# Turning the merged branches of three column groups on VectorE and through DRAM instead of on TensorE

## The chip, the cores and the metric

One NeuronCore of a Trainium2 chip runs the whole program. The metric is the time of one execution in microseconds; the kernel before has a median of 1301.43 us over three runs (1301.05 to 1301.47). Engines are named as in the profile: PE is TensorE, ACT is ScalarE, DVE is VectorE, POOL is GpSimd, SP is SyncE (here it only issues DMAs). The program holds one list of instructions for each engine, and the listings and timelines below follow these lists.

## The reference, cut to what matters

One layer of a hybrid streaming encoder over 512 positions (S) and 2048 channels (D). Three attention branches give ys, one gating path gives gates, and the layer ends with

```python
up = jnp.einsum('bsnw,nwd->bsnd', ys, w_up)       # 3 branches, 512 -> 2048 columns each
merged = jnp.sum(gates * up, axis=2)              # (1, 512, 2048)
return x + jnp.einsum('bsd,de->bse', merged, w_out)
```

The change touches only the step between the last two lines: `merged` is produced with positions on the partitions, and the product with w_out contracts over its columns, so it must be turned (transposed) before TensorE can use it.

## The kernel before, in words

**Products.** All large products are made in float32 from pairs of rounded parts: an operand is split into a high part (ACT copies it to fp32r, lines 247 and 376) and a low part (DVE subtracts the high part, lines 251 and 386), and three products high-high, low-high and high-low are added in PSUM. All of them are issued in line 266. A *unit* is the work on one loaded piece of weights, 512 KB (`raw`, loaded on SP in line 278): ACT makes `wh`, DVE makes `wl`, PE multiplies. There are three buffers for `wh` and two for `wl`, so DVE can make the `wl` of a unit only when the unit two before it is finished.

**The stage around the change.** `up_units` (line 1312) makes the up-projection by column groups g of 512 columns, in the order 0, 2, 1, 3. In each group the branches C, B, A come one after the other, two units each, so six units to a group. A unit does its work by blocks of 128 positions (tb = 0 to 3): four products with `wh`, two with `wl`. After the second unit of a branch has finished a block, `taken` (lines 1319 to 1333) lets DVE multiply the block's PSUM bank by the gate (L1323, `sg<-acc,sg`), which also frees that bank, and, for branches B and A, add it to `merged` (L1330). There are four such banks (`acc`), one for each tb, so the first unit of the next branch can start its block tb only when L1323 of the same tb has read the bank.

**Turning.** When the four blocks of a group are merged, `turned_m` (line 1350) turns 128 columns at a time: four PE transposes into one PSUM bank (L1357), an ACT copy to SBUF (L1364, `m<-att`). Sixteen transposes and four copies to a group. The copy `m` goes to `merged_a` for groups 0 and 1 (DVE subtracts halves in L1378, then the split of lines 247 and 251) or to `merged_b` for groups 2 and 3 (DVE L257 several times, then splits). After the four groups, `out_task` makes the product with w_out in a Strassen form, whose operands are these splits.

**What sets the order.** The order on PE, ACT and DVE is fixed while the program is built, by a planner (`Flow`, line 65). Every piece of work is a generator that yields what it waits for and what it costs on which engine; the planner keeps a clock for each engine, takes the piece that could start first, and the instructions are recorded in that order (`manual_schedule`). SP's and POOL's DMAs are recorded when the planner passes them. Three rules of it matter here. A generator that yields an `Event` whose time is already known runs on at once, with its own `ready` set to that time. `spawn(gen, slack, ready)` starts a new generator with the `ready` that it is given. `flow.fin` is the end of the piece of work that was planned last. At run time nothing of the planner is left but the order; each instruction waits on semaphores for what it really needs.

**DMA semaphores.** DMAs on SP use eight semaphores in turn (DMAHW0 to DMAHW7 in the listings), and a DMA waits for the one before it on its semaphore.

**A round trip that the kernel has already.** `gate` (line 913) turns the 128x512 gate tile of a head with four DVE transposes of 128x128 (L920, each in blocks of 32x32), one store to DRAM (L923, `gd<-gt`) and four loads issued on ACT (L930, `g<-gd`, 64 KB each), which put the blocks in their places.

Of the kernel before, what the change touches and what calls it, by code (L numbers as in the profile page):

```python
# [8 lines left out]
F32 = mybir.dt.float32  # L9
# [6 lines left out]
P = 128  # L16
S = 512
# [4 lines left out]
NB = 3  # L22
KT = D // P
QB = S // P
DT = D // P
UK = 8
CH = 4
NQ = 4
# [9 lines left out]
PE, ACT, DVE = 0, 1, 2  # L38
# [26 lines left out]
class Flow:  # L65
# [16 lines left out]
    def give(self, slots, n=1):  # L82
        slots.free += [self.fin] * n

    def spawn(self, gen, slack, ready=None):
        task = Task(gen, slack, self.now if ready is None else ready)
        self.tasks.append(task)
        self.advance(task)
# [66 lines left out]
def act_us(n, x=1):  # L155
    return x * (0.075 + 0.00095 * n)


def dve_us(n, x=1):
    return x * (0.1 + 0.00105 * n)  # L160
# [3 lines left out]
def hybrid_kernel(  # L164
# [13 lines left out]
    nc = tc.nc  # L178
# [7 lines left out]
    dp = ctx.enter_context(tc.tile_pool(name="dp", bufs=1, space=bass.MemoryType.DRAM))  # L186
# [9 lines left out]
    flow = Flow()  # L196
    spawn, set_, give = flow.spawn, flow.set, flow.give
    t2s, atts, raws, xps = Slots(NT, KEPT), Slots(4), Slots(NR), Slots(NX)
    accs, wls = Slots(4), Slots(LA)

    def t2(s, dt=F32):
        return tp.tile([P, S], dt, tag="t2", name=nm(s))
# [7 lines left out]
    def att():  # L210
        return pt.tile([P, S], F32, tag="att", name=nm("att"))
# [4 lines left out]
    def blk(i):  # L216
        return slice(i * P, (i + 1) * P)
# [3 lines left out]
    def two(ap):  # L221

        return ap.rearrange("p (h s) -> p h s", h=2)
# [20 lines left out]
    def split(hi, lo, src, n, ev=None, due=(), hi_ev=None):  # L244

        yield (ACT, act_us(n), *due)
        nc.scalar.activation(hi, src, AF.Copy)  # L247
        if hi_ev is not None:
            set_(hi_ev)
        yield (DVE, dve_us(n), *due)  # L250
        nc.vector.tensor_sub(lo, src, f(hi))
        if ev is not None:
            set_(ev)

    def minus(to, a, b):

        nc.vector.scalar_tensor_tensor(to, a, -1.0, b, op0=ALU.mult, op1=ALU.subtract)  # L257
# [83 lines left out]
    units = []  # L341
    side = {}

    def at(u, g, slack=5.0):
        side.setdefault(u, []).append((g, slack))
# [471 lines left out]
    class Head:  # L817
# [306 lines left out]
        def stages(self):  # L1124

            one = lambda fn, i: lambda: fn(i)
            if self.n == C:
                s, t, o = OFF["cs"], OFF["ct"], OFF["co"]
                g = [(0, one(self.qk, K)), (0, one(self.qk, Q)), (s - 1, self.stick_start)]
                g += [(s + i, one(self.stick_scores, i)) for i in range(QB)]  # L1130
            else:
                s, t, o = (OFF["s1"], OFF["t1"], OFF["o1"]) if self.last else (OFF["s"], OFF["t"], OFF["o"])
                g = [(0, self.norms), (1, one(self.qk, K)), (2, one(self.qk, Q)), (s - 2, self.soft_start)]
# [166 lines left out]
    def gates_of(n, g, tb):  # L1300
        yield last_head.event("hl", 2)
        yield t2s, 1
        t = sig[n, g, tb] = t2("sg")
        yield fetch(t, gl[n, g, tb], flow.now, 256)
        yield last_head.event("g")
        yield ACT, act_us(S) + 0.1
        nc.scalar.activation(t, t, AF.Sigmoid)
        set_(sig_ev[n, g, tb])

    merged, merged_ev = {}, {}  # L1310

    def up_units(g, b):
        n = (C, B, A)[b]
        ps = [None] * QB
        for tb in range(QB):
            sig_ev[n, g, tb] = Event()
            merged_ev[b, g, tb] = Event()

        def taken(tb):
            yield sig_ev[n, g, tb]  # L1320
            t = sig[n, g, tb]
            yield DVE, dve_us(S)
            nc.vector.tensor_mul(t, ps[tb], t)  # L1323
            give(accs)
            if b == 0:
                merged[g, tb] = t
            else:
                yield merged_ev[b - 1, g, tb]
                yield DVE, dve_us(S)
                nc.vector.tensor_add(merged[g, tb], merged[g, tb], t)  # L1330
                give(t2s)
            set_(merged_ev[b, g, tb])

        def mms(i):
            def block(k, tb):
                y = b * NH + 2 * i + k
                return ys[y] and (*ys[y].block(tb), y_ev[y])

            def go(u):
                yield from products(u, ps, (0, 1), range(QB), block, i == 0, i == 1, None if i else (accs, acc),  # L1340
                                    done=taken, outer=True)
            return go

        return [Unit(mms(i), srcs=[w_up[g, b, i]]) for i in range(2)]
# [2 lines left out]
    m4_ev = [Event() for _ in range(UK // 2)]  # L1347
    kept_m, m1_ev, mus = {}, [Event() for _ in range(UK)], {}

    def turned_m(g, i):  # L1350
        for tb in range(QB):
            yield merged_ev[NB - 1, g, tb]
        yield atts, 1
        yield PE, 0.11 * QB
        ps = att()
        for tb in range(QB):
            nc.tensor.transpose(ps[:, blk(tb)], merged[g, tb][:, blk(i)], identf)  # L1357
        turns[g] = turns.get(g, 0) + 1
        if turns[g] == QB:
            give(t2s, QB)  # L1360
        yield t2s, 1
        yield ACT, act_us(S)
        m = t2("m")
        nc.scalar.activation(m, ps, AF.Copy)  # L1364
        give(atts)
        k = 4 * g + i
        if k < UK:
            kept_m[k] = m
            spawn(merged_a(k, m), 4.0, flow.fin)
        else:  # L1370
            spawn(merged_b(k - UK, m), 3.0, flow.fin)

    turns = {}

    def merged_a(k, a):

        yield DVE, dve_us(HS)
        nc.vector.tensor_sub(a[:, RH], a[:, LH], a[:, RH])  # L1378
        yield xps, 1
        m1[k] = Parts("m1", [m1_ev[k]] * 2)  # L1380
        yield from split(m1[k].hi, m1[k].lo, two(a), S, m1_ev[k])

    def merged_b(k, b):
        a = kept_m[k]
        yield m1_ev[k]
        yield t2s, 1
        t = t2("mt")
        if k % 2 == 0:
            yield t2s, 1
            mus[k // 2] = t2("mu")  # L1390
        u = mus[k // 2][:, RH if k % 2 else LH]
        q = DVE, dve_us(HS)
        yield q
        minus(t[:, LH], b[:, RH], a[:, RH])
        yield q
        minus(t[:, RH], t[:, LH], a[:, LH])
        give(t2s)
        yield q
        minus(u, t[:, LH], b[:, LH])
        yield xps, 1  # L1400
        ev = Event()
        m23[k] = Parts("m23", [ev, ev])
        yield from split(m23[k].hi, m23[k].lo, two(t), S, ev)
        give(t2s)
        if k % 2 == 0:
            yield xps, 1
            m4[k // 2] = Parts("m4")
            set_(m4_ev[k // 2])
        yield xps, 1
        ev = Event()  # L1410
        m2[k] = Parts("m2", [ev, ev])
        yield from split(m2[k].hi, m2[k].lo, two(b), S, ev)
        give(t2s)
        yield m4_ev[k // 2]
        h, lo, ev = m4[k // 2].half(k % 2)
        yield from split(h, lo, u, HS, ev)
        if k % 2:
            give(t2s)

    for g in (0, 2, 1, 3):  # L1420
        for b in range(NB):
            for tb in range(QB):
                at(len(units) - (3 - tb // 2 if g or b else 2), lambda n=(C, B, A)[b], g=g, tb=tb: gates_of(n, g, tb))
            units.extend(up_units(g, b))
        for i in range(QB):
            at(len(units) - 1, lambda g=g, i=i: turned_m(g, i))
    for b in range(NB):
        at(len(units) - 2 * (NB - 1 - b), freed(xps, NH))

# [90 lines left out]
NX = 28  # L1520
NR = 8

OFF = dict(cs=4, ct=12, co=14, s=8, t=14, o=16, s1=3, t1=4, o1=5)
FAT, FGAP, FLATE = 44, 15, 3.5

# [48 lines left out]
```

## Time and profile before

| | us |
|---|---|
| median of three runs | 1301.43 |
| span of the profiled execution | 1300.1 |
| PE busy | 1294.1 (100%) |
| DVE busy | 1069.5 (82%) |
| ACT busy | 748.2 (58%) |

The profiled execution is one of its own; the page lists its span from the first to the last instruction, 1.3 us below the median of the runs. A row of a timeline holds the start, the time, the engine, the line, the operation, the tile written and the tiles read, and how many instructions were merged into the row; in square brackets stands the idle time ahead of it and what ended it. DMA rows give the bytes of one transfer and the median time from issue to landing.

### The profile page before, as it was taken

What the parts mean: (1) busy time and instruction counts of PE and PEld (TensorE: products, weight loads), DVE (VectorE), ACT (ScalarE), POOL (GpSimd) and SP (SyncE); (2) the same over time, 40 slices, a digit from 0 to 9 for tenths busy, and PEclk for the clock granted to TensorE, in tenths of its full rate; (3) what the DMA queues carried; (4) which work ended last, traced back from release to release, by engine and by line L of the source; (5) the groups of instructions that cost most, each with busy time, mean ns of one, the idle gap of its engine ahead of it and who ended that gap; (6) DMA issues with size and microseconds to landing.
All of it is one profiled execution on the core that took longest, in us unless ns stands there. A gap on an engine that the chain in (4) does not pass through costs nothing.

```text
span 1300.1 us, 17368 instructions
## 1 busy us (share of the span) xinstructions
PE 1294.1 (100%) x5941; PEld 1075.1 (83%) x5941; DVE 1069.5 (82%) x1607; ACT 748.2 (58%) x1259; POOL 92.0 (7%) x116
## 2 busy tenths in 40 slices
PE   9999999999999999999999999999999999999998
PEld 8888888888888888888888888888888888888887
DVE  7966797898989888898886886978879668698767
ACT  7745465565557646576466664666658546463442
POOL 0001000110011001110011000110000000000110
PEclk9999999999999999999999999999999999999999
DMA  9855687896788989888787777877796756738983
GB/s 358 256 147 145 185 230 194 230 239 215 218 238 237 250 236 272 236 240 240 205 249 175 222 213 191 252 162 208 224 282 194 264 194 196 177 93 258 250 245 126
DMA packets 124072, 284.39 MB, mean 219 GB/s; under 512 B 34368, under 2 KB 40144, under 8 KB 123984
## 3 DMA queue, kind: packets, MB, share of 16 engines
q1 hardware_dynamic: 83328, 221.42, 50.7%
q0 software_dynamic: 14976, 54.53, 23.1%
q10 hardware_dynamic: 25680, 7.34, 2.3%
q8 instruction: 46, 0.75, 0.2%
q14 instruction: 42, 0.34, 0.1%
HBM read 260.66 MB, written 22.59 MB: 218 GB/s over the span
## 4 chain that ended last, share of the span: by engine, by line
PE 99%; DMA 1%; DVE 0%; issue 0%; ACT 0%; ACTq 0%
PE acc L266 93%; PE att L1019 1%; PE att L873 1%; DMA gl<-u 1%; PE att L1109 1%; PE att L1108 1%; PE att L261 1%; PE att L262 1%; PE att L263 1%; PE att L1357 1%; PE att L1107 1%; PE att L430 0%; DVE s L702 0%; DVE u L1161 0%; DVE gt L920 0%
## 5 line engine op out<-in xcount | busy, mean ns | idle before, releaser
L376 ACT ACTIVATE wh<-raw 128x1024 fp32r<-128x1024 f32 (+1 forms) x404 | 426.9, 1057 | 412.6 <-PE acc L266 317.6
L386 DVE TENSOR_TENSOR wl<-raw,wh 128x1024 fp32r<-128x1024 f32 (+1 forms) x405 | 492.6, 1218 | 159.1 <-PE acc L266 110.6
L266 PE MATMUL acc<-wh,x 128*128 128x512 f32 x1664 | 428.7, 392 | 0.1
L266 PEld LDWEIGHTS acc<-wh,x 128*128 128x128 f32 x1664 | 310.2, 188 | 62.8 <-issue 0.3
L266 PE MATMUL acc<-wh,t 128*128 128x512 f32 x1056 | 272.4, 391 | 0.0
L266 PE MATMUL acc<-wl,x 128*128 128x512 f32 x832 | 230.7, 391 | 0.0
L266 PEld LDWEIGHTS acc<-wh,t 128*128 128x128 f32 x1056 | 197.1, 188 | 40.3
L266 PEld LDWEIGHTS acc<-wl,x 128*128 128x128 f32 x832 | 155.4, 188 | 32.3 <-DVE wl L386 0.2
L266 PE MATMUL acc<-wl,t 128*128 128x512 f32 x528 | 148.0, 392 | 0.0
L282 POOL DMA_DIRECT2D raw<-in_w_col x88 | 76.1, 865 | 867.6 <-ACT wh L376 209.0
L588 DVE TENSOR_TENSOR raw<-raw,raw 128x1024 f32<-128x1024 f32 x104 | 126.4, 1218 | 0.1
L266 PEld LDWEIGHTS acc<-wl,t 128*128 128x128 f32 x528 | 98.3, 188 | 19.7
L266 PE MATMUL acc<-wh,m 128*128 128x512 f32 x448 | 112.9, 389 | 0.0
L266 PE MATMUL acc<-wh,y 128*128 128x512 f32 x384 | 103.1, 390 | 0.0
L266 PEld LDWEIGHTS acc<-wh,m 128*128 128x128 f32 x448 | 84.1, 188 | 17.4
L266 PEld LDWEIGHTS acc<-wh,y 128*128 128x128 f32 x384 | 72.0, 188 | 15.0
L266 PE MATMUL acc<-wl,m 128*128 128x512 f32 x224 | 62.5, 390 | 0.0
L266 PE MATMUL acc<-wl,y 128*128 128x512 f32 x192 | 59.5, 391 | 0.0
L266 PEld LDWEIGHTS acc<-wl,m 128*128 128x128 f32 x224 | 41.9, 188 | 8.8 <-DVE wl L386 0.2
L266 PEld LDWEIGHTS acc<-wl,y 128*128 128x128 f32 x192 | 35.8, 188 | 7.1
L247 ACT ACTIVATE ah<-att 128x512 fp32r<-128x512 f32 (+3 forms) x48 | 20.9, 436 | 31.7 <-PE att L1019 31.6
L1323 DVE TENSOR_TENSOR sg<-acc,sg 128x512 f32<-128x512 f32 x48 | 32.9, 690 | 5.0 <-PE acc L266 2.6
(182 smaller groups left out, 1119.9 us busy)
## 6 DMA issues: line engine op xcount, KB each, us to landing
raw<-in_w_col SPq DMA_DIRECT2D x235, 512.0 KB, 5.0
raw<-in_w_col POOLq DMA_DIRECT2D x88, 512.0 KB, 8.2
raw<-in_w_out SPq DMA_DIRECT2D x40, 512.0 KB, 4.1
raw<-in_w_up SPq DMA_DIRECT2D x24, 512.0 KB, 3.8
sg<-gl SPq DMA_DIRECT2D x48, 256.0 KB, 4.8
xf<-in_xn SPq DMA_DIRECT2D x32, 256.0 KB, 6.7
raw<-in_w_out POOLq DMA_DIRECT2D x16, 512.0 KB, 6.5
gl<-u SPq DMA_DIRECT2D x22, 256.0 KB, 9.9
```

The costliest lines, as they stand in the source:

```text
L247: nc.scalar.activation(hi, src, AF.Copy)
L261: nc.tensor.matmul(ps, lh, rh, start=start, stop=False, skip_group_check=more)
L262: nc.tensor.matmul(ps, lh, rl, start=False, stop=False, skip_group_check=more)
L263: nc.tensor.matmul(ps, ll, rh, start=False, stop=stop, skip_group_check=more)
L266: nc.tensor.matmul(ps, w, x, start=start, stop=stop, skip_group_check=more)
L282: nc.gpsimd.dma_start(to, src, accum_op=ALU.add)
L376: nc.scalar.activation(u.hi, u.raw, AF.Copy)
L386: nc.vector.tensor_sub(u.lo, u.raw, f(u.hi))
L588: nc.vector.tensor_add(to.raw, to.raw, self.raw)
L873: nc.tensor.transpose(ps[:, blk(tb)], self.c[tb][:, blk(r)], identf)
L1019: nc.tensor.transpose(ps[:, blk(i)], self.p[i][:, blk(j)], identf)
L1323: nc.vector.tensor_mul(t, ps[tb], t)
```

## The change

For the column groups in `DRAMS = (0, 2, 1)`, that is all but the last, `turned_m` is replaced. `folded(g, tb)` transposes each merged 128x512 block in place on DVE (in 32x32 blocks, L1356) and stores it to DRAM on SP (L1359, 256 KB). The new `turned_m(g, i)` then loads each of the four turned tiles with four DMAs on SP (L1373, 64 KB each, rows of 128 bytes), 16 loads to a group, and passes the tile to `arrived`, which starts `merged_a` or `merged_b`. Group 3 keeps the PE transposes (`spun_m`).

```diff
+    def folded(g, tb):
+        yield merged_ev[NB - 1, g, tb]
+        m = merged[g, tb]
+        yield DVE, dve_us(S) + 0.07
+        nc.vector.transpose(m, m)
+        if g not in md:
+            md[g] = dp.tile([QB, P, S], F32, name=nm("md"))
+        nc.sync.dma_start(md[g][tb], m)
+        stored(t2s, 1, 256)
+        md_ev[g, tb].t = t2s.free[-1] + MLATE
...
     def turned_m(g, i):
+        for tb in range(QB):
+            yield md_ev[g, tb]
+        yield t2s, 1
+        m = t2("m")
+        q = md[g].rearrange("t (a r) c -> (t a) r c", r=32)
+        for b in range(4):
+            c = i * P + 32 * b
+            nc.sync.dma_start(m[32 * b:32 * (b + 1), :].rearrange("p (n c) -> p n c", c=32),
+                              q[:, :, c:c + 32].rearrange("n r c -> r n c"))
+        yield Event(landing(flow.fin, 512) + 1.0)
+        arrived(g, i, m)
+
+    def arrived(g, i, m):
+        k = 4 * g + i
+        if k < UK:
+            kept_m[k] = m
+            spawn(merged_a(k, m), 4.0, flow.fin)
+        else:
+            spawn(merged_b(k - UK, m), 3.0, flow.fin)
...
         for i in range(QB):
-            at(len(units) - 1, lambda g=g, i=i: turned_m(g, i))
+            if g in DRAMS:
+                at(len(units) - 1, lambda g=g, i=i: folded(g, i))
+                at(len(units) - 1 + MSKIP, lambda g=g, i=i: turned_m(g, i))
+            else:
+                at(len(units) - 1, lambda g=g, i=i: spun_m(g, i))
...
+DRAMS = (0, 2, 1)
+MLATE, MSKIP = 2.5, 1
```

The instructions move as follows. In the listings a row is one instruction: line, operation, tile written, tiles read, and the semaphores that it waits for (DMAHW are SP's DMAs, PE_49, DVE_49 and Activation_49 the engines). `wl_9691` before and `wl_9684` after are the same low part, that of the third unit of group 2; `sg_9481` and `sg_9483` are the blocks 0 and 1 of branch C of group 2.

First DVE, before, at the end of group 0, from the last merged block on:

```order
L1330 TENSOR_TENSOR sg_9361<-sg_9361,sg_9436 128x512 [waits DVE_49]
L386 TENSOR_TENSOR wl_9614<-raw_9204,wh_9570 128x1024 [waits DMAHW4_49,Activation_49]
L1378 TENSOR_TENSOR m_9642<-m_9642 128x256 [waits Activation_49]
L1378 TENSOR_TENSOR m_9649<-m_9649 128x256 [waits Activation_49]
L251 TENSOR_TENSOR m_1905_9657<-m_9642,m_1905_9657 128x2x256 [waits Activation_49]
L251 TENSOR_TENSOR m_1906_9661<-m_9649,m_1906_9661 128x2x256 [waits Activation_49]
L1378 TENSOR_TENSOR m_9676<-m_9676 128x256 [waits Activation_49]
L386 TENSOR_TENSOR wl_9691<-raw_9228,wh_9612 128x1024 [waits DMAHW5_49,PE_49]
L1378 TENSOR_TENSOR m_9692<-m_9692 128x256 [waits Activation_49]
L1323 TENSOR_TENSOR sg_9481<-acc_9613,sg_9481 128x512 [waits PE_49]
```

and the same place after the change (one transpose of the four, that of block 0, stands four rows further up):

```order
L1330 TENSOR_TENSOR sg_9361<-sg_9361,sg_9436 128x512 [waits DVE_49]
L386 TENSOR_TENSOR wl_9616<-raw_9204,wh_9570 128x1024 [waits DMAHW4_49,Activation_49]
L1356 STREAM_TRANSPOSE sg_9357<-sg_9357 128x512
L1356 STREAM_TRANSPOSE sg_9359<-sg_9359 128x512
L1356 STREAM_TRANSPOSE sg_9361<-sg_9361 128x512 [waits DVE_49]
L1409 TENSOR_TENSOR m_9656<-m_9656 128x256 [waits DMAHW2_49,DMAHW7_49,DMAHW1_49,DMAHW0_49]
L386 TENSOR_TENSOR wl_9684<-raw_9228,wh_9614 128x1024 [waits DMAHW5_49,PE_49,Activation_49]
L1409 TENSOR_TENSOR m_9661<-m_9661 128x256 [waits DMAHW5_49,DMAHW6_49,DMAHW4_49,DMAHW3_49]
L1323 TENSOR_TENSOR sg_9481<-acc_9615,sg_9481 128x512 [waits PE_49]
L1409 TENSOR_TENSOR m_9666<-m_9666 128x256 [waits DMAHW2_49,DMAHW7_49,DMAHW1_49,DMAHW0_49]
L1409 TENSOR_TENSOR m_9671<-m_9671 128x256 [waits DMAHW5_49,DMAHW6_49,DMAHW4_49,DMAHW3_49]
L1323 TENSOR_TENSOR sg_9483<-acc_9626,sg_9483 128x512 [waits PE_49]
```

The subtractions on the turned tiles (L1378 before, L1409 after) keep their place behind the group's end; what they wait for has become the landing of four DMAs, and they stand ahead of `wl_9684` and of both L1323.

SP at the end of group 0, after the change (before, the eight loads `sg<-gl` followed directly on the `raw` load):

```order
L1359 DMA md_9603<-sg_9355 128x512 [waits DMAHW2_49,DVE_49]
L278 DMA raw_9633<-in_w_up 128x1024 [waits DMAHW3_49,DVE_49]
L1359 DMA md_9603<-sg_9357 128x512 [waits DMAHW4_49,DVE_49]
L1359 DMA md_9603<-sg_9359 128x512 [waits DMAHW5_49,DVE_49]
L1359 DMA md_9603<-sg_9361 128x512 [waits DMAHW6_49,DVE_49]
L1373 DMA m_9656<-md_9603 32x16x32 [waits DMAHW6_49,DMAHW5_49,DMAHW7_49,DMAHW4_49,DMAHW2_49]
L1373 DMA m_9656<-md_9603 32x16x32 [waits DMAHW0_49]
L1373 DMA m_9656<-md_9603 32x16x32 [waits DMAHW1_49]
```

The first load of the first tile waits for all four stores; thirteen more loads follow these rows, and then the gates `sg<-gl` of a later branch.

DVE at the end of group 1, the third, after the change; the `wl` of the third unit of group 3 (`wl_10286`) and block 0 (`sg_10089`) stand ahead of the waits here, blocks 1 and 2 (`sg_10111`, `sg_10132`) behind them:

```order
L386 TENSOR_TENSOR wl_10286<-raw_9868,wh_10231 128x1024 [waits PE_49]
L1323 TENSOR_TENSOR sg_10089<-acc_10232,sg_10089 128x512 [waits PE_49]
L1409 TENSOR_TENSOR m_10292<-m_10292 128x256 [waits DMAHW6_49,DMAHW7_49,DMAHW1_49,DMAHW0_49]
L1323 TENSOR_TENSOR sg_10111<-acc_10243,sg_10111 128x512 [waits PE_49]
L1409 TENSOR_TENSOR m_10297<-m_10297 128x256 [waits DMAHW4_49,DMAHW5_49,DMAHW3_49,DMAHW2_49]
L1409 TENSOR_TENSOR m_10302<-m_10302 128x256 [waits DMAHW6_49,DMAHW7_49,DMAHW1_49,DMAHW0_49]
L1409 TENSOR_TENSOR m_10307<-m_10307 128x256 [waits DMAHW4_49,DMAHW5_49,DMAHW3_49,DMAHW2_49]
L1323 TENSOR_TENSOR sg_10132<-acc_10257,sg_10132 128x512 [waits PE_49]
```

Before, four blocks of L1323 stood there behind four subtractions that waited for ACT alone. At the end of group 2 the order is that of group 0 with L257 in place of L1409, except that two tiles stand ahead of block 0, the third ahead of block 3, and the fourth behind all blocks.

More of the change, by code (lines that the diff above doesn't have):

```diff
@@ L1348, in hybrid_kernel, with spun_m @@
     kept_m, m1_ev, mus = {}, [Event() for _ in range(UK)], {}
-    def turned_m(g, i):
+    md = {}
+    def folded(g, tb):
[8 more added lines that the diff above has]
+        md_ev[g, tb].t = t2s.free[-1] + MLATE
+    md_ev = {(g, tb): Event() for g in range(NQ) for tb in range(QB)}
+    def turned_m(g, i):
+        for tb in range(QB):
[16 more added lines that the diff above has]
+            spawn(merged_b(k - UK, m), 3.0, flow.fin)
+    def spun_m(g, i):
         for tb in range(QB):
@@ L1365, in turned_m @@
         give(atts)
[L1366 to L1371, printed above, removed]
+        arrived(g, i, m)
     turns = {}
```

## The prediction

> **What bounds the kernel now.** I read the page first, then the chain that ended last. PE is busy for the whole span.
>
> ```profile
> span 1300.1 us, 17368 instructions
> PE 1294.1 (100%) x5941; PEld 1075.1 (83%) x5941; DVE 1069.5 (82%) x1607; ACT 748.2 (58%) x1259; POOL 92.0 (7%) x116
> PE 99%; DMA 1%; DVE 0%; issue 0%; ACT 0%; ACTq 0%
> ```
>
> So what is taken from PE is won, and what makes PE wait is lost, one for one; other engines count only where PE waits for them. The chain in order of time shows the stage of the change:
>
> ```profile
> 1014.76 26.37 PE acc L266 x116
> 1041.13 1.75 PE att L1357 x16
> 1042.87 32.69 PE acc L266 x144
> 1075.56 1.75 PE att L1357 x16
> 1077.31 32.66 PE acc L266 x144
> 1109.97 1.75 PE att L1357 x16
> ```
>
> Sixteen transposes take 1.75 us of PE after each group, with no gap around them. How much time the others have follows from PE's timeline after group 0. Each pair of rows `wh x4`, `wl x2` is one block.
>
> ```profile
> 1038.69 1.07 PE L266 MATMUL acc<-wh,y 128*128 128x512 f32 x4
> 1039.60 0.62 PE L266 MATMUL acc<-wl,y 128*128 128x512 f32 x2
> 1040.05 1.08 PE L266 MATMUL acc<-wh,y 128*128 128x512 f32 x4
> 1040.96 1.91 PE L1357 MATMUL att<-identf,sg 128*128 128x128 f32 x16
> ...
> 1045.93 1.07 PE L266 MATMUL acc<-wh,y 128*128 128x512 f32 x4
> ...
> 1051.37 1.07 PE L266 MATMUL acc<-wh,y 128*128 128x512 f32 x4
> ```
>
> Group 2 starts at 1038.69. A block takes 1.36 us, a unit 5.44 (1045.93 to 1051.37). Without the 1.75 us its unit 2 starts at 1044.18 and unit 3 at 1049.62. Unit 3 needs two things of DVE. Its block tb writes the bank that branch C's block tb held, so L1323 of that block must be over: block 0 at 1049.6, block 1 at 1051.0, block 2 at 1052.3. And its `wl` must be there 0.9 us after its start.
>
> **Removed.** 48 transposes in three groups, 3 x 1.75 = 5.25 us of PE: all of it counts, as PE has no gap there. The twelve ACT copies go too (L1364, off the path, so nothing).
>
> **Added on DVE.** Twelve transposes of 128x512. The trace has only those of 128x128, beside other full tiles.
>
> ```profile
> 62.83 0.88 DVE L920 STREAM_TRANSPOSE gt<-c 128x128 f32<-128x128 f32 x4
> ...
> 1038.89 0.69 DVE L1323 TENSOR_TENSOR sg<-acc,sg 128x512 f32<-128x512 f32 x1
> 1039.61 0.69 DVE L1330 TENSOR_TENSOR sg<-sg,sg 128x512 f32<-128x512 f32 x1
> 1040.22 1.22 DVE L386 TENSOR_TENSOR wl<-raw,wh 128x1024 fp32r<-128x1024 f32 x1
> 1042.23 0.91 DVE L1378 TENSOR_TENSOR m<-m 128x256 f32<-128x256 f32 x2 [0.79 <-ACT m L1364]
> ```
>
> Four small ones take 0.88 us, so one large one is at most that; if it runs by elements like the other 128x512 rows it is 0.65 (their step on DVE). I take 0.65, as four times the elements of 0.22 minus three starts comes near it. The last merged block is written at 1040.3. The first transpose pushes this chain to 1040.95, the `wl` of unit 2 to 1042.1 (PE wants it at 1045.1, so it is covered), and the three other transposes end at 1044.0. All this fits into DVE's idle time; if nothing else came it would cost nothing.
>
> **Added: the round trip, and the wait for it.** The order shows that the subtractions on the loaded tiles (L1409 m_9656 to m_9671) stand right behind the transposes on DVE. The builder placed them there because `yield Event(landing(...))` holds nothing up once the time is known, and `arrived` gives its child `flow.fin` as ready time: the landing isn't in the child's account. DVE now waits there, and behind it are queued `wl_9684` of unit 3 and L1323 of blocks 0 to 3, for which PE waits. How long? The nearest DMA rows:
>
> ```profile
> raw<-in_w_up SPq DMA_DIRECT2D x24, 512.0 KB, 3.8
> gl<-u SPq DMA_DIRECT2D x22, 256.0 KB, 9.9
> g<-gd ACTq DMA_DIRECT2D x44, 64.0 KB, 2.9
> yd<-y SPq DMA_DIRECT2D x11, 256.0 KB, 4.4
> gl<-c SPq DMA_DIRECT2D x4, 256.0 KB, 2.0
> ...
> L930 ACTq DMA_DIRECT2D g<-gd x44: 309/500/608, 75.9 to 925.8; - x44
> DMA to landing us min/median/max: 1.9/2.9/8.3
> ...
> 75.88 2.06 ACTq L930 DMA_DIRECT2D g<-gd  x4
> ...
> 1024.00:1026.00 2.00, 2.00 (x11) 1.65 (x10) 1.95 (x3) 0.65 (x2) 0.00 (x0) 1.00 1.05 406
> 1038.00:1040.00 2.00, 2.00 (x10) 1.68 (x9) 1.93 (x4) 1.06 (x1) 0.00 (x0) 1.00 0.00 0
> ```
>
> A store of this shape lands 2.0 to 9.9 us after its issue; which, depends on the DMA traffic, and here it is low (the last row but one is a full stretch, 406 GB/s; the last, at the group's end, has none). In the way are one `raw` load and the group's own stores, 512 + 768 KB from 1042.7 on, 3.2 us at 406 GB/s; with some 1.3 us of fixed delay (2.0 less 0.65 for 256 KB) the last store, issued at 1044.1, lands at 1047.2, 3.1 us later. Then 16 loads at 0.5 us of SP each, landing 1.9 to 2.9 after issue (I take 2.2 for the quiet queue): the four tiles are there at 1050.9, 1052.9, 1054.9 and 1056.9. SP's semaphores, eight in turn, do not bind, as eight issues last 4 us.
>
> DVE after group 0, with 0.4 for a subtraction, 1.2 for a `wl` and 0.65 for L1323: tile 1 at 1051.3, `wl` at 1052.5, tile 2 at 1053.3, block 0 freed at 1053.95. PE starts unit 3 at 1054.05 instead of 1049.6: **4.45 us lost**. Its block 0 lasts to 1055.4; block 1 is behind tiles 3 and 4, freed at 1057.95: **2.65 more**. Blocks 2 and 3 then come in time.
>
> After group 2 only tile 1, the `wl` and tile 2 stand ahead of block 0, and no wait follows: **4.5**. DVE is denser there, so up to 0.8 more, which I leave to the range.
>
> After group 1 the `wl` and block 0 stand ahead of the waits. The transposes end at 1045.0 on the same scale, as one more split lies between them, and the tiles come 0.5 later: block 1 is freed at 1052.5 (**1.6**), block 2, behind tiles 2 to 4, at 1058.5 against 1053.95 (**4.6**).
>
> The sum: 7.1 + 4.5 + 6.2 = 17.8 us lost, 5.25 won: +12.6. Against the profiled span this is 1312.7; the median lies 1.3 above the span, so 1314.0. Semaphore steps and group 2's density are left out of this and only add (L1323 starts at 1038.89, 0.2 after PE's block ended at 1038.69; some six such steps lie on the path), so I say **1315**.
>
> The ends: with the fastest rows (store 2.0, load 1.9, issue 0.31) the same walk gives 2.9 + 2.0 + 2.5 = 7.4 lost, +2.2, 1303.6. With the store at 9.9 and the load at 2.9 each group loses 7.5 more: 1337. With 4.4 (the row `yd`) it is 1.3 more for each group, 1318.
>
> **Moved on SP.** Behind the waits stand the next gates and weights. The gates `sg_9679` on go out at 1056 instead of 1042, but serve branch A, units 5 and 6, from about 1073 on even with the waits; a `raw` load is due 40 us before use. POOL's loads are not passed. The twelve stores and 48 loads move 6 MB, about 16 us of DMA at 406 GB/s in 105 us, in stretches that are partly idle: nothing, unless they delay each other, which the upper end holds.
>
> **A rule that speaks against the change.** The loads put 128-byte rows to their places by access pattern. The Trainium skill, "VectorE: DVE Perf Modes", section "The three transpose paths", warns that a plain DMA that transposes by strides can be 19 times slower than the crossbar's 1309 ns; by that, as an estimate, a load would take some 25 us and the change would cost over 60 us. The rows of `g<-gd`, the same 128-byte pieces, have 2.9 us, so here the trace decides against the rule.
>
> **Rivals.** (a) *The round trip is hidden*, and the kernel is faster: 1301.4 - 5.25 = 1296.2. For it: DVE has idle time in every unit. It decides at the tile landings: tile 2 would have to be there by 1048.5, 4.5 us after the last transpose, and tile 4 by 1049.9. The fastest rows give 1050.2 and 1052.7, so it needs something faster than any row. 0.05. (b) *Fast landings*: 1302 to 1309, by the lower end above. 0.14. (c) *Slow landings*: DMA queues fill, as in the head stage (9.9 for `gl<-u`): 1321 to 1337. 0.10. (d) *PE runs slower after a long wait.* The start of the trace is the only place after a pause:
>
> ```profile
> 5.25 2.77 PE L266 MATMUL acc<-wh,x 128*128 128x512 f32 x8
> 7.85 1.10 PE L266 MATMUL acc<-wl,x 128*128 128x512 f32 x4
> 8.79 2.00 PE L266 MATMUL acc<-wh,x 128*128 128x512 f32 x8
> 10.62 1.07 PE L266 MATMUL acc<-wl,x 128*128 128x512 f32 x4
> ```
>
> Twelve products take 3.54 us there and the next twelve 2.74, so a restart costs about 0.8; at three to five waits of over 2 us that is 2 to 4 us: 1317 to 1319, inside the forecast's range. If the loss is three times that, 1321 to 1327. 0.08. The Trainium skill, "TensorE: Matmul & The Clock Gate", section "What's actually happening", says that an idle window of about 3.4 us halves the clock until a busy window has passed; by it, as an estimate, each wait of 4.5 us could cost 1.7 us more, 5 us in all and 1320. No trace here shows a wait of that length within the run. (e) *The change does little*: the order shows the 48 PE transposes gone, so "nothing happens" could only be waits that cancel the gain, 1298.8 to 1304.0. 0.05 beyond what (b) puts there.
>
> **How the numbers follow.** My forecast, the walk above within 1309 to 1321, has 0.58; the rivals (a) to (e) have 0.05, 0.14, 0.10, 0.08 and 0.05. The range leaves out (a), most of (e), some of (b) and the upper halves of (c) and (d): 1305 to 1327. A measurement of this kernel tells 0.2%, 2.6 us, from no change. Faster by more than that is (a), 0.05; within it is (e) and the lowest part of (b), 0.07; slower is the rest, 0.88.
>
> **What would show it right or wrong.** In the profile after: L1357 at 16 instead of 64; L1356 at 0.65 us; in the waits new groups "DVE L1409 and L257 <- DMA m", 5 to 7 us at their longest, and "PE <- DVE sg L1323" two to three times of 2 to 5 us, just before unit 3 of groups 2, 1 and 3. PE's span there is three gaps of 7, 4.5 and 6 us. It is wrong if PE keeps no gap, if the gap comes from another line (`wh`, `sg<-gl`), or if the round trip is clearly shorter than 7 us from transpose to first tile.

## The result and the profile after

| | us |
|---|---|
| before, median of 4 runs | 1301.45 (1301.05 to 1302.35) |
| after, median of 4 runs | 1331.18 (1329.32 to 1333.04) |
| ratio | 1.023, 95% interval 1.0215 to 1.0244 |
| span of the profiled execution after | 1329.8 (29.7 more than before) |

The kernel is slower, by about twice what was forecast (+29.7 us measured, +13.6 forecast), and lies 4 us above the range. The page of after, with the shares of the chain that ended last:

```profile
span 1329.8 us, 17382 instructions
PE 1299.4 (98%) x5893; PEld 1074.9 (81%) x5893; DVE 1075.4 (81%) x1619; ACT 743.1 (56%) x1247; POOL 91.7 (7%) x116
PE 92%; DVE 3%; DMA 3%; SPq 1%; issue 0%; DVEq 0%
```

48 PE instructions fewer, yet PE is 5.3 us *longer* busy, and the chain, 99% PE before, now also goes through DVE, DMA and SP. The waits say who waits for whom (in all, times, longest):

```profile
DVE m L1409 <- DMA m<-md: 27.9, 8, 8.2
PE acc L266 <- DVE sg L1323: 18.7, 4, 5.9
DVE mt L257 <- DMA m<-md: 9.1, 2, 8.2
PE acc L266 <- ACT m L247: 5.7, 1, 5.7
```

These are the groups that the prediction named, but for the last. That one is the first wait after group 0; ACT's L247 there waits for DVE's L1409, and DVE's L1323 of block 0, which PE needs too, runs from 1054.42 to 1055.10, so it would have held PE to the same point (1055.25). The stage in order of time, first PE after group 0 and at the later restarts:

```profile
1048.05 1.07 PE L266 MATMUL acc<-wh,y 128*128 128x512 f32 x4
...
1055.25 2.05 PE L266 MATMUL acc<-wh,y 128*128 128x512 f32 x4 [5.68 <-ACT m L247]
...
1060.61 1.34 PE L266 MATMUL acc<-wh,y 128*128 128x512 f32 x4 [2.46 <-DVE sg L1323]
...
1062.60 1.91 PE L266 MATMUL acc<-wh,y 128*128 128x512 f32 x4
...
1065.07 1.08 PE L266 MATMUL acc<-wh,y 128*128 128x512 f32 x4
...
1066.46 1.08 PE L266 MATMUL acc<-wh,y 128*128 128x512 f32 x4
...
1099.75 2.04 PE L266 MATMUL acc<-wh,y 128*128 128x512 f32 x4 [5.92 <-DVE sg L1323]
...
1141.42 2.08 PE L266 MATMUL acc<-wh,y 128*128 128x512 f32 x4 [4.50 <-DVE sg L1323]
...
1150.15 2.08 PE L266 MATMUL acc<-wh,y 128*128 128x512 f32 x4 [5.80 <-DVE sg L1323]
```

Without a wait, unit 3 after group 0 would start at 1049.41 (1048.05 + 1.36) and unit 4 at 1054.85; unit 4 starts at 1066.46, so this group costs 11.6 us. Block 1 starts 9.84 late (1060.61 against 1050.77), which is waiting; the other 1.8 are blocks that run slowly: 1060.61 to 1062.60 and 1062.60 to 1065.07, 1.99 and 2.47 us instead of 1.36. (Block 0 was slow too, but that is hidden in the wait behind it.) The same reckoning, over rows of which only the first after each wait is shown, gives 9.1 us after group 2 (6.1 waiting, 3.0 slow blocks) and 13.8 after group 1 (12.0 and 1.8). The sum is 34.5; less the 5.25 of the transposes it is 29.3, against 29.7 in the spans.

Why PE waits that long is in the chain of after, group 0's end and then the end of group 1:

```profile
1043.65 4.26 DMA md<-sg
1048.06 0.33 SPq L1373
...
1055.88 3.53 DMA m<-md
1059.53 0.42 DVE m L1409
1059.96 0.61 DVE sg L1323
1060.61 18.27 PE acc L266 x72
...
1130.48 5.86 DMA md<-sg
...
1142.10 1.68 SPq L1373
...
1146.48 2.47 DMA m<-md
```

The chain runs through the last store (4.26 us), sixteen load issues one behind the other, the landing of the last load (3.53) and DVE's in-order list to the L1323 that frees the bank. What the transfers took is read from one stretch of time and then from the rows over all three groups, with the lines on landing under the two DMA rows:

```profile
1043.00:1048.00 5.00, 5.00 (x24) 4.14 (x23) 0.63 (x2) 1.06 (x1) 0.00 (x0) 1.00 0.78 255
```

This is the stretch in which the last three stores of group 0 and the `raw` load issued just ahead of them are under way (the last value is GB/s, the one before it the DMA share). The first store, issued alone at 1038.08, landed in 2.0 us; these three, issued from 1042.47 on, took 4.2 to 4.3 us each. After group 1, between loads of w_out, all four took 5.8 to 6.0.

```profile
L1356 DVE STREAM_TRANSPOSE sg<-sg x12: 669/686/706, 1037.3 to 1129.8; 128x512 f32<-128x512 f32 x12
```

```profile
L1359 SPq DMA_DIRECT2D md<-sg x12: 319/326/602, 1038.1 to 1130.5; - x12
...
DMA to landing us min/median/max: 2.0/4.4/6.0
```

```profile
L1373 SPq DMA_DIRECT2D m<-md x48: 318/487/1683, 1048.1 to 1146.5; - x48
...
DMA to landing us min/median/max: 2.0/2.6/5.9
```

And the slow blocks: the granted clock (eighth value, after POOL's) in stretches around the waits of group 0. The values ahead of it are the length of the stretch and the busy time of PE, PEld, DVE, ACT and POOL, with the number of instructions.

```profile
1054.80:1058.10 3.30, 2.85 (x6) 1.83 (x6) 0.73 (x2) 0.99 (x2) 0.00 (x0) 0.50 0.83 139
1058.20:1061.50 3.30, 0.89 (x4) 0.75 (x5) 1.97 (x4) 1.51 (x3) 0.00 (x0) 1.00 0.93 292
1061.60:1064.90 3.30, 3.30 (x9) 2.51 (x9) 3.30 (x6) 0.49 (x1) 0.00 (x0) 0.50 0.96 336
1065.00:1068.40 3.40, 3.40 (x16) 2.77 (x16) 1.89 (x3) 2.15 (x4) 0.00 (x0) 1.00 0.70 261
```

After both waits PE works at half clock: it makes 6 products in the 3.3 us from 1054.80 on and 9 from 1061.60 on, against 16 in the 3.4 us from 1065.00 on, at 1.00. The Trainium skill, "TensorE: Matmul & The Clock Gate", section "What's actually happening", says that an idle window of about 3.4 us halves the clock; the 0.50 after the wait of 5.68 us agrees. The second time the clock falls after a wait of 2.46 us only, in a stretch that was not all idle (PE busy for 0.89 of 3.30 us), so here the trace goes beyond that rule.

### The profile page after: what moved, and what is told of

It reads as the page before. It is cut to its first block, busy times and chain, and to the rows that moved or that the text cites. A ratio compares the mean times of both kernels' runs of the same rounds, so it can differ in the third digit from the quotient of the medians.

```text
span 1329.8 us, 17382 instructions
## 1 busy us (share of the span) xinstructions
PE 1299.4 (98%) x5893; PEld 1074.9 (81%) x5893; DVE 1075.4 (81%) x1619; ACT 743.1 (56%) x1247; POOL 91.7 (7%) x116
## 4 chain that ended last, share of the span: by engine, by line
PE 92%; DVE 3%; DMA 3%; SPq 1%; issue 0%; DVEq 0%
PE acc L266 87%; SPq L1373 1%; DMA md<-sg 1%; PE att L1019 1%; DMA gl<-u 1%; PE att L873 1%; DVE sg L1323 1%; DMA m<-md 1%; PE att L1108 1%; PE att L1109 1%; DVE sg L1356 1%; PE att L262 1%; PE att L1107 1%; PE att L263 1%; DVE sg L1330 1%; PE att L261 1%
## 5 line engine op out<-in xcount | busy, mean ns | idle before, releaser
L266 PE MATMUL acc<-wh,y 128*128 128x512 f32 x384 | 109.8, 409 | 24.4 <-DVE sg L1323 18.7
L266 PEld LDWEIGHTS acc<-wh,y 128*128 128x128 f32 x384 | 75.6, 199 | 43.1 <-DVE sg L1323 14.6
L247 ACT ACTIVATE ah<-att 128x512 fp32r<-128x512 f32 (+3 forms) x48 | 20.9, 436 | 31.7 <-PE att L1019 31.6
L282 POOL DMA_DIRECT2D raw<-in_w_out x16 | 13.8, 863 | 316.7 <-DVE sg L1330 167.1
```

The source lines that it names most:

```text
L266: nc.tensor.matmul(ps, w, x, start=start, stop=stop, skip_group_check=more)
L282: nc.gpsimd.dma_start(to, src, accum_op=ALU.add)
```

## The experiments

Two questions: is the order on DVE, which takes no account of the landings, the whole loss, and can the round trip be hidden at all? And what is the share of the clock? Times are medians; each has a before measured with it (1301.01 for numbers 1 to 4, 1300.86 for 5 to 8, 1300.72 for 9 to 11, 1300.58 for 12). The ratio and its interval are taken over all runs of both kernels and need not be the quotient of the two medians. Line numbers shift by one where a line was added (L1410 is L1409); in the two filled kernels L1328 is L1323.

**1. The transposes without the trip.** DVE's transposes stay; store and loads are replaced by ACT copies, so the 32x32 blocks are left out of place and the product is not the reference's.

```diff
-        nc.sync.dma_start(md[g][tb], m)
...
-            nc.sync.dma_start(m[32 * b:32 * (b + 1), :].rearrange("p (n c) -> p n c", c=32),
-                              q[:, :, c:c + 32].rearrange("n r c -> r n c"))
+        nc.scalar.activation(m, merged[g, i], AF.Copy)
```

> The twelve DVE transposes stay and the PE transposes of three groups stay away, but the tiles do not go through DRAM: ACT copies each turned block from SBUF (the blocks are not put in their places, so the turning is left incomplete and the output is not the reference's). The order theory (DVE's list holds waits for landings ahead of what PE needs) and its rival (DRAM traffic and the busy SP queue slow the stage whatever the order) both give 5.25 us below before, 1296.2. If the DVE transposes themselves were what PE waits for, it would be 1303 or more.

Measured: 1297.55 us, ratio 0.9974 (0.9963 to 0.9984). That is 3.5 us below before, 1.3 short of what was expected: PE has one wait of over 1 us in the stage, 1.33 us on L1323. So the transposes on DVE are not the loss; it hangs on the trip, or on what the lists do with it (this kernel changes both).

**2. The planner is told when the tiles land.** The child starts in the planner's account at the planned end of the four stores plus 2.1 us for each tile plus 2.0. The stores and loads of the trip stay as they are, and in front of group 0's loads stands the same as in after but for one weight load; what changes is the order on DVE and ACT, and on SP that of some weights and gates behind.

```diff
-        yield Event(landing(flow.fin, 512) + 1.0)
-        arrived(g, i, m)
+        landing(flow.fin, 512)
+        arrived(g, i, m, max(md_ev[g, tb].t for tb in range(QB)) + 2.1 * (i + 1) + MWAIT)
...
-            spawn(merged_a(k, m), 4.0, flow.fin)
+            spawn(merged_a(k, m), 4.0, ready)
...
-MLATE, MSKIP = 2.5, 1
+MLATE, MSKIP, MWAIT = 2.5, 1, 2.0
```

> All transfers as in the changed kernel; only the planner is told when the tiles land, so the subtractions stand later in DVE's list. Order theory: PE keeps no gap, 1296 to 1299. Rival (transfers whatever the order): stores and loads still cost, 1315 to 1331.

Measured: 1302.0 us, ratio 1.0008 (0.9998 to 1.0017), no measurable difference from before. The time lies 3 us above the theory's band and far below the rival's. The 5 to 6 us waits and the slow blocks are gone (clock 1.000), with the trip itself unchanged (its stores and loads land 4.4 and 2.6 us after issue by the median, as in after): nearly the whole loss of 29.7 us was the order in the lists. But no gain is left either. PE keeps two waits of over 1 us, 1.80 after group 0 and 1.10 after group 1. What holds PE after group 0 shows on ACT and PE:

```profile
1058.85 0.63 ACT L1307 ACTIVATE sg<-sg 128x512 f32<-128x512 f32 x1 [9.92 <-DMA sg<-gl]
...
1060.33 0.61 ACT L247 ACTIVATE m<-m 128x512 fp32r<-128x512 f32 x1
```

```profile
1062.33 1.20 PE L266 MATMUL acc<-wh,y 128*128 128x512 f32 x4 [1.80 <-DVE sg L1323]
```

```profile
1047.02 8.95 SPq L1373 DMA_DIRECT2D m<-md  x16
1056.01 1.91 SPq L278 DMA_DIRECT2D sg<-gl  x4
```

The gates leave SP only behind the sixteen loads, at 1056.01. ACT waits 9.92 us for the first with its sigmoid, and behind the sigmoid stand a `wh` (1059.38) and the split L247 of the first turned tile; behind L247, on DVE, stand L251 and the L1323 for which PE waits.

**3. PE kept busy in its waits.** As after, with repeated products into a spare bank at the five places where PE waited, so that the clock has no idle window.

```diff
+                    if fill is not None and fill(tb):
+                        junk_ps = att()
+                        for _ in range(fill(tb)):
+                            mm(junk_ps, block(kts[0], tb)[0], u.hi[:, 0, :], True, True)
...
+FILL = {(2, 1, 0): 24, (2, 1, 1): 16, (1, 1, 0): 25, (3, 1, 1): 19, (3, 1, 2): 31}
```

> The changed kernel with 115 products repeated into a spare PSUM bank just where PE waits (24 and 16 in group 2, 25 in group 1, 19 and 31 in group 3), so that PE is busy for most of each wait; the lists of DVE, ACT and SP are unchanged and the output too. The wait theory with a clock share of 6.6 us (PE's slow blocks after the last wait of each group: 1.8 + 3.0 + 1.8) gives 1324.6. If the clock has no share on the path, 1331; if the whole excess of 16.7 us over the predicted waits were clock, 1314.5.

Measured: 1327.26 us, ratio 1.0218 (1.0187 to 1.0249), clock 1.000 in the profiled execution, and the block after the longest wait left runs at full speed:

```profile
1139.59 1.19 PE L266 MATMUL acc<-wh,y 128*128 128x512 f32 x4 [2.22 <-DVE sg L1328]
```

All the other blocks of the stage do too, with the lists of DVE, ACT and SP as in after. So the slow blocks come from PE's idleness and not from DVE or the DMAs. The size is not shown this way: the median is 3.9 us below that of after, where the slow blocks were 6.6, but the four runs go from 1326.62 to 1335.83, and the interval of the ratio overlaps that of after. In two places the filling outlasted the wait.

**4. Only group 0.** `DRAMS = (0,)`, all else as after.

> Only group 0 goes through DRAM, groups 2, 1 and 3 keep the PE transposes. If each group pays for itself: 11.6 lost less 1.75 won, 1301.45 + 9.9 = 1311.3. If the loss builds up over the groups (DMA queues filling, buffers running short), less than a third of 29.7: below 1309.

Measured: 1311.62 us, ratio 1.0084 (1.0069 to 1.0099): +10.6, against 9.9 worked out from after's first group (11.6 - 1.75). Group 0 alone pays its own loss; that groups 2 and 1 do the same is read from after's rows, not from runs of their own.

**5. Less filling**, to end inside each wait:

```diff
+FILL = {(2, 1, 0): 22, (2, 1, 1): 9, (1, 1, 0): 20, (3, 1, 1): 22, (3, 1, 2): 24}
```

> As e3_pe_filled with fewer repeated products where the filling there ended after DVE had freed the bank (22 and 9 in group 2, 20 in group 1, 22 and 24 in group 3); output unchanged. In e3 the slow blocks were gone and 3.9 us were won, with about 0.95 us lost where the filling of block 1 in group 2 outlasted the wait. If the clock's share is the 6.6 us of slow blocks, 1324.6 here, less than e3 by 1 to 2.5; if it is smaller than that and the landings make the rest, no less than e3's 1327.3.

Measured: 1330.2 us, ratio 1.0222 (1.0207 to 1.0238): the 1324.6 failed. The other number, no less than 1327.3, fits, but not for its reason: the clock fell again. The same places had other waits than in number 3, and in one the rest of the wait was long enough:

```profile
1137.85 1.19 PE L266 MATMUL acc<-wh,y 128*128 128x512 f32 x4 [2.34 <-DVE sg L1328]
1148.54 2.08 PE L266 MATMUL acc<-wh,y 128*128 128x512 f32 x4 [3.58 <-DVE sg L1328]
```

Here 2.34 us of idleness left the clock alone and 3.58 halved it. What the clock costs in all is read from after's blocks (6.6 us); as a difference of times these two runs don't settle it.

**6. The loads two units later, the landings still not in the account.** `MSKIP = 3`.

> The changed kernel with MSKIP 3 for 1: the same account of landings (none), but the turned tiles are asked for two units later, so the subtractions stand behind the L1323 of branch C in DVE's list, at a point where the stores have landed. Order theory: the stores' 4.4 us are hidden and only the loads' landing is waited for, one wait of 2 to 4 us in each group, partly covered: 1300 to 1312. Rival (transfers whatever the order): 1325 or more.

Measured: 1313.97 us, ratio 1.0098 (1.0083 to 1.0113), above the expected band by 2 us. Pushing the whole task back hides more than half of the loss, but the waits only move:

```profile
1062.88 1.31 PE L266 MATMUL acc<-wh,y 128*128 128x512 f32 x4 [3.50 <-DVE sg L1323]
1140.48 2.04 PE L266 MATMUL acc<-wh,y 128*128 128x512 f32 x4 [10.35 <-ACT sg L1307]
```

**7 and 8. The loads on POOL's queue**, on top of number 2, so that SP's gates need not stand behind them; number 8 for groups 0 and 2 alone.

```diff
-            nc.sync.dma_start(m[32 * b:32 * (b + 1), :].rearrange("p (n c) -> p n c", c=32),
+            nc.gpsimd.dma_start(m[32 * b:32 * (b + 1), :].rearrange("p (n c) -> p n c", c=32),
```

> e2_ready with the 48 loads of the turned tiles issued on POOL instead of SP, so SP's list (gates and weights of the next branches) is not held up. In e2 ACT waited 9.9 us for a gate that SP issued 14 us later than before, and PE waited 1.8 us behind it. If SP's held-up list is what e2 still loses, 1298 to 1300; if it is the density of DVE (twelve more transposes) or the loads' traffic, 1302 as in e2.

> e7 with groups 0 and 2 alone through DRAM; group 1, whose round trip falls together with the first loads of w_out (stores landed after 5.9 us there), keeps the PE transposes: 1.75 us of the gain is given up. If group 1's traffic costs more than that, this is faster than e7; if not, slower by up to 1.75.

Measured: 1306.16 (1.0043, 1.0028 to 1.0058) and 1305.76 us (1.0043, 1.0028 to 1.0057). Number 7 missed both of its numbers: it is slower than number 2. Number 8 does not differ from it measurably. The loads land 6.6 us after issue from POOL (median, number 7), against 2.6 from SP in after, and PE's wait of 2.12 us in number 7 hangs on such a landing (between the two rows of the chain stand L1410, splits, a `wl` and L1323 on DVE):

```profile
m<-md POOLq DMA_DIRECT2D x48, 64.0 KB, 6.6
```

```profile
1061.00 8.18 DMA m<-md
...
1073.41 12.75 PE acc L266 x48
```

This failed for a cost of its own, landings later than the account has them, and decides nothing on the gates.

**9, 10 and 11. Number 2 with the loads two units later** (`MSKIP = 3`): for groups 0, 2 and 1, for group 0, and for groups 0 and 2.

```diff
-DRAMS = (0, 2, 1)
-MLATE, MSKIP = 2.5, 1
+DRAMS = (0, 2, 1)
+MLATE, MSKIP, MWAIT = 2.5, 3, 2.0
```

> As the run with the real ready times in the planner's account, but the loads of the turned tiles are planned two units later, so that on SP six of the eight gate loads of a later branch go out ahead of a group's sixteen loads instead of behind them. Theory (what is left after the landings are accounted for is the gates that come late behind the sixteen loads, and with them the ACT and DVE work that is queued behind the sigmoid): the waits of 1 to 2 us on PE go, and the kernel comes near the run without the trip, 1297.5 to 1299.5. Rival (DVE's density in these units is what is left, the gates are not): 1301 to 1303, with waits on L1323 of the same size.

> The same rules, but only the first group takes the round trip and the other three use the PE transposes. Its gain is at most 1.75 us of PE. If the late gates were what was left: 1299.3 to 1300.3. If DVE's density is what is left: group 0 is followed by a group with the most idle time on DVE, so 1300 to 1301, no measurable change.

> The same rules with the first two groups on the round trip; their loads meet neither the w_out weights nor POOL's accumulating loads. At most 3.5 us of PE are won. If the late gates were what was left: 1297.9 to 1299.5, as good as three groups or better. If DVE's density is: 1299.5 to 1301.

Measured: **1296.18 us for three groups, ratio 0.9965 (0.9952 to 0.9977), faster than before** and 1.3 us below the band that was expected; 1299.82 for one (0.9993, 0.9984 to 1.0002), 1297.44 for two (0.9975, 0.9965 to 0.9984). That is 4.5, 0.9 and 3.3 us of the 5.25, 1.75 and 3.5 that the transposes take; the 0.9 alone is not clear of no change. DVE's density, the rival, is out: the same twelve transposes stand in this list. The page's span and the chain of three groups, where the whole stage is one piece of PE:

```profile
span 1293.6 us, 17386 instructions
```

```profile
1013.08 124.74 PE acc L266 x550
```

And DVE's wait for the tiles, 27.9 + 9.1 us in after and 5.4 in number 2:

```profile
DVE m L1410 <- DMA m<-md: 0.8, 1, 0.8
```

On SP the sixteen loads of group 0 still go out in one run, at 1046.37; two gates went ahead of them, not six as the expectation says. ACT shows what is different from number 2:

```profile
1048.60 0.61 ACT L1307 ACTIVATE sg<-sg 128x512 f32<-128x512 f32 x1
1053.08 1.06 ACT L376 ACTIVATE wh<-raw 128x1024 fp32r<-128x1024 f32 x1 [3.86 <-PE acc L266]
1054.04 0.61 ACT L247 ACTIVATE m<-m 128x512 fp32r<-128x512 f32 x1
1058.41 0.64 ACT L1307 ACTIVATE sg<-sg 128x512 f32<-128x512 f32 x1 [3.75 <-DMA sg<-gl]
```

The early gates' sigmoids are done in time, a `wh` and the split of the first tile come next, and only then the sigmoid that waits for a gate behind the loads.

**12. Number 2 with the gates one unit earlier**, the loads where they were. On SP the same two gates come ahead of group 0's loads as in number 9.

```diff
-                at(len(units) - (3 - tb // 2 if g or b else 2), lambda n=(C, B, A)[b], g=g, tb=tb: gates_of(n, g, tb))
+                at(len(units) - (4 - tb // 2 if g or b else 2), lambda n=(C, B, A)[b], g=g, tb=tb: gates_of(n, g, tb))
```

> As the run with the real ready times in the planner's account, with one other edit than the run with late loads: the turned tiles' loads are planned where they were, and the gates of a branch are planned one unit earlier. On SP this puts the same two gate loads ahead of the first group's sixteen loads as in the run with late loads. Theory (what was left were the gates that came late behind the sixteen loads, with the sigmoid, wh and the splits queued behind them on ACT): no wait of over 0.5 us after group 0, 1296 to 1298.5 in all. Rival (the late loads gained by another order of the splits on DVE, and the gates had no part): 1300.5 to 1302.5 with the wait of 1.8 us after group 0 still there.

Measured: 1298.73 us, ratio 0.9985 (0.9976 to 0.9994). Each side has half: the time is nearer to the theory's, but the wait after group 0 is still there, as the rival said.

```profile
1059.50 0.63 ACT L1307 ACTIVATE sg<-sg 128x512 f32<-128x512 f32 x1 [10.03 <-DMA sg<-gl]
...
1060.99 0.61 ACT L247 ACTIVATE m<-m 128x512 fp32r<-128x512 f32 x1
```

```profile
1062.98 1.21 PE L266 MATMUL acc<-wh,y 128*128 128x512 f32 x4 [1.91 <-DVE sg L1323]
```

So two gates ahead of the loads are not enough: with all gates one unit earlier, ACT's list again has the sigmoid of a late gate ahead of L247. In numbers 2 and 12 that order goes with the wait, in number 9 the other order goes without it. That it is this order alone is read from the rows; no kernel changed it by itself, and number 9 has another order of the splits on DVE too.

## Why the prediction was wrong

- **PE bounds, and 5.25 us are to be won: right.** Number 9 has 4.5 of them.
- **DVE's transposes fit in (0.65 us each): right**, 0.686 measured, and number 9, with all twelve, has no wait on PE in the stage.
- **DVE stands at the subtractions because the planner's account lacks the landings, and PE waits for L1323 behind them, in three places: right.** The waits name these lines, and number 2 takes the loss away with the same stores and loads.
- **The size of the waits: wrong, and the term that failed is the landing of the transfers.** The prediction's "which, depends on the DMA traffic, and here it is low" was read from a stretch of before without the trip's own stores. The bytes in the way were counted right: 255 GB/s over 5.00 us are about the 512 + 768 KB. But they were put at 406 GB/s, 3.2 us. The stores, put at 3.1 us from issue to landing, took 4.26, 4.48 and 5.86 on the chain; the last load after group 0, put at 2.2, took 3.53. After group 1 the sixteen load issues stretched as well, from 7.8 us between the first and the last (group 0) to 10.0, with one issue of 1.68, and weights of the next product (issued on SP at 1127.80 and 1131.62) were under way with the stores. Waits of 7.1, 4.5 and 6.2 us became 9.8, 6.1 and 12.0: 10.1 us more in all. A store beside its neighbours and a weight load was rather the 4.4 us of `yd<-y`, which stood among the ends as 1318.
- **A slip in the walk**: after group 1 the transposes were said to end at 1045.0, 1.0 later than after group 0, and the tiles to come 0.5 later. With 1.0 the forecast's sum would be 0.5 us more, which changes nothing.
- **A load by strides at some 25 us, the rule set aside: rightly.** The 48 loads landed in 2.6 us by the median, near the 2.9 of `g<-gd`.
- **The clock: left out of the sum and priced too low.** This is the second term that failed. Rival (d) took 0.8 us per restart from the first products of the trace. Those follow no wait within the run; measured are 1.8, 3.0 and 1.8 us beyond what the waits hide, 6.6 in all. The estimate beside it, 1.7 for each wait, was the nearer one.
- **These two terms are the whole error**: 10.1 + 6.6 = 16.7, and 12.6 + 16.7 = 29.3, against 29.7 measured. Each was a rival of its own, (c) and (d). The 1331.18 falls into the band of (c), 1321 to 1337, but not by its reason alone: no store on the chain took the 9.9 us that its upper end is made of, and without the 6.6 us of slow blocks the rows give 1324.6. The case that both come together had no place, though both hang on the same long waits.
- **"Moved on SP: nothing": wrong, but hidden in after by the larger waits.** When the gates are used was reckoned from the product that needs them (1073). But ACT's list has the sigmoid earlier, with other work behind it. It became visible in number 2, as the next wait once the first was gone.
- **Rival (a), the hidden round trip**, was rightly held unlikely for the order as it was. With the landings in the account alone it did not come either (number 2, 1302.0); it needed the later loads as well (number 9). That its 1296.2 and the 1296.18 of number 9 agree is partly luck: beside its own before number 9 wins 4.5 us, not 5.25.

## What to carry to other kernels

Where the order is fixed at build time, every wait that the planner doesn't know is paid by all that stands behind it; put the landing in the account before judging a change of engine. Price a wait of several us on PE with its slow restart (1.8 to 3.0 us here), and a round trip with the DMAs that the change itself puts beside it. When the first wait is gone look for the next one on each in-order list, ACT's and SP's too, before calling the change worthless.

## What was not expected of the hardware

- The clock goes by more than the length of one wait. A wait of 2.55 us in number 8 left it alone, while after one of 2.12 in number 7 the block ran slowly:

```profile
1115.05 1.21 PE L266 MATMUL acc<-wh,y 128*128 128x512 f32 x4 [2.55 <-DVE sg L1323]
```

```profile
1073.41 1.88 PE L266 MATMUL acc<-wh,y 128*128 128x512 f32 x4 [2.12 <-DVE sg L1323]
```

In after's trace the granted clock changes around group 0 at 1054.7, 1058.1, 1061.5 and 1064.9, which is 3.4 us apart each time, though the two waits end at 1055.25 and 1060.61. That suggests that where a wait lies among these steps counts too; no run here was made to test it.
- The same 64 KB loads land 6.6 us after issue from POOL (number 7) and 2.6 from SP (after), by the medians.
- One issue on SP, 0.49 us by the median, took up to 1.68 after group 1, where some of the loads landed 5.6 to 5.9 us after issue instead of 2.6; which of the two is the cause of the other is not shown.
